# Decoder layers in f32 with seven-product pairs: one weight sum made by an accumulating transfer, wider VectorE instructions, a third such pair in the long down products

## The chip, the cores and the metric

The kernel runs on one core of a Trainium2 chip. The metric is the device time of one execution, in microseconds. Engines are named as the profile names them: PE (TensorE) with its weight loads (PEld), DVE (VectorE), ACT (ScalarE), POOL (GpSimd) and SP (SyncE). DVE, ACT, POOL and SP each work through their own instructions in order.

## The reference

Two decoder layers on one sequence of 256 tokens of width 2048, all in float32. Layer 0 mixes tokens by dilated window attention, layer 1 by multi-head latent attention; both then run a SwiGLU feed-forward block (FFN), with RMS norms ahead of each and one at the end. The change lies in the FFN:

```python
D_MODEL = 2048; SEQ = 256; FFN_HIDDEN = 5632
def swiglu(xn, w_gu, w_down):
    g, u = jnp.split(xn @ w_gu, 2, axis=-1)
    return (jax.nn.silu(g) * u) @ w_down
...
h = h + swiglu(rms_norm(h, ffn_norm_g[layer]), ffn_w_gu[layer], ffn_w_down[layer])
```

## The kernel before

**Products.** Each f32 number is split into a high part `hi` (a rounding to TensorE's fast f32 form) and a rest `lo`, and each product is three matmuls, hi x hi, hi x lo and lo x hi (`mul`, L689 to L691). Activations are split once, weights as they arrive.

**The weight stream.** `WeightStream` brings weights in units of 1 MB (128 partitions x 2048 numbers). `load` issues a unit's transfers on SP into one of three `raw` buffers; `split` casts `hi` on ACT (L167) and subtracts `lo` on DVE (L168), into one of three pairs of buffers. `next`, called as TensorE's code for a unit is written, first writes the split two units ahead and then the load that this frees a buffer for. So the order on each engine is that of the program text, and a load waits until DVE has finished with the buffer.

**Units.** A unit of the FFN is a 2 x 2 set of 512-column blocks (two blocks of the inner dimension, two output columns: gate and up, or two columns of the down product) for two 128-token halves. An "eight" makes its eight block products straight, 24 matmuls. A "seven" makes the same by a scheme of Strassen's kind from seven products, 21 matmuls, with sums of weights (`th`, `tl`, after four DVE instructions at L185 to L188 on the raw tile) and sums of activations (`forms` for the gate/up products, `forms_h` for the down products, both built by `sums`, L662 to L667). The results of the sevens of a group gather in four PSUM banks `pb` beside the accumulators `la` and `ra`, and are combined at the group's end by a copy on ACT (L718) and four adds on DVE (L721) into the tiles `gate` and `up` (`left` and `right` in `mixed`).

**Groups.** The hidden dimension (44 tiles of 128) is worked in parts of 16, 16 and 12. A part has a group of eight units for every 4 tiles of gate and up, 11 groups a layer; units 2, 4 and 6 of a group are sevens (`SEVEN`), but not in the first group of a layer. A part of 16 then has two down groups of eight units, of which 2 and 5 are sevens (`SEVEN_DOWN`); the part of 12 ends in plain products (`product`). After a gate/up group, DVE adds the accumulators to `gate` and `up` (L739), ACT makes the silu (L745) and DVE the product with `up` (L747, two instructions). The transposes of that result, eight on PE (L405), are put off by one unit (`later`), so that they stand right behind unit 0 of the next group. After a down group DVE adds into `h` (L763), and POOL issues two accumulating transfers of 512 KB that add `left` and `right` to `h` (L766). POOL does nothing else in the FFN but two powers of norms (L420).

`across` (L434 to L439) turns a per-token factor into a row, once or twice a layer, by way of a diagonal tile.

Of the kernel before, what the change touches and what calls it, by code (L numbers as in the profile page):

```python
# [45 lines left out]


SEVEN = (2, 4, 6)
SEVEN_DOWN = {16: (2, 5), 12: ()}


def shape_constants():
# [35 lines left out]
class WeightStream:  # L88
# [81 lines left out]
    def split_blocks(self, raw, form):  # L170

        hi, lo = [self.hl_pool.tile([P, 2048], F32R, tag=n, name=n, bufs=self.ahead + 1) for n in ("hi", "lo")]
        blk = lambda t, i: t[:, i * 512:(i + 1) * 512]
# [9 lines left out]
        tt(out=b22, in0=b22, in1=b12, op=ALU.subtract)  # L185
# [37 lines left out]
def kernel(ctx, tc, consts, x, attn_norm_g, ffn_norm_g, a_w_qkv, a_w_o, kv_norm_g,  # L223
# [205 lines left out]

    def across(r, name):  # L430

        dg = tmp.tile([P, S], F32, tag="diag", name="diag", bufs=1)
        for t in range(NT):
            nc.vector.tensor_scalar(out=dg[:, t * P:(t + 1) * P], in0=ident, scalar1=r[:, t:t + 1],  # L434
                                    scalar2=None, op0=ALU.mult)
        ps = bank()
        mm(out=ps[:, :S], lhsT=ones, rhs=dg, start=True, stop=True)
        R = small.tile([P, S], F32, name=name, tag=name, bufs=1)
        nc.vector.tensor_copy(out=R, in_=ps[:, :S])  # L439
        return R  # L440

# [199 lines left out]
    def ffn(xT, rstd, finish):  # L641

        with tc.tile_pool(name="ffn", bufs=1) as fp:
# [11 lines left out]
            forms_h = fp.tile([P, 2, 2, 3, P], F32R, name="forms_h")  # L655

            def sums(x, kp, d):


                x2 = x[:, 2 * kp:2 * kp + 2, :].bitcast(F32)  # L660
                f = tmp.tile([P, 2, S], F32, tag="t1", name="f")
                nc.vector.tensor_tensor(out=f, in0=x2[:, :, 0:S], in1=x2[:, :, S:2 * S], op=ALU.add)  # L662
                (a11, a21), (a12, a22) = [[f[:, k, t * P:(t + 1) * P] for t in range(NT)] for k in range(2)]
                g = tmp.tile([P, 4, P], F32, tag="t1", name="g")
                for i, x_, y_, op in ((0, a21, a22, ALU.add), (1, g[:, 0], a11, ALU.subtract),
                                      (2, a11, a21, ALU.subtract), (3, a12, g[:, 1], ALU.subtract)):
# [12 lines left out]
            def mixed(X, pairs, seven, sums_of, left, right):  # L679
# [2 lines left out]


                la, ra = acc_tile(), acc_tile()
                pb = None
# [7 lines left out]
                for kp in range(pairs):  # L693
                    w = ws.next()
                    x = lambda t, kk: [X[:, 2 * kp + kk, o + t * P:o + (t + 1) * P] for o in (0, S)]
                    if kp in seven:
# [3 lines left out]
                            pb = [bank() for _ in range(4)]  # L700
                        y = lambda j: x(1, 0) if j == 0 else [sums_of[:, i, h, j - 1, :] for h in range(2)]
                        mul(pb[0], x(0, 0), w[:2], 1, st, sp)
                        mul(la[:, 0], x(0, 1), w[:2], 3, False, False)
                        mul(ra[:, 0], y(3), w[:2], 2, False, False)
                        mul(la[:, 1], x(1, 1), w[2:], 3, False, False)
                        mul(pb[1], y(0), w[2:], 0, st, sp)
                        mul(pb[2], y(1), w[2:], 1, st, sp)
                        mul(pb[3], y(2), w[2:], 2, st, sp)
                    else:
                        st, sp = kp == 0, kp == pairs - 1  # L710
                        for acc, n in ((la, 1), (ra, 0)):
                            for t in range(NT):
                                mul(acc[:, t], x(t, 0), w, n, st, False)
                                mul(acc[:, t], x(t, 1), w, n + 2, False, sp)
                    later.tick()
                    if seven and kp == seven[-1]:
                        u2 = fp.tile([P, 512], F32, tag="u2", name="u2")
                        nc.scalar.copy(out=left[:, 0], in_=pb[0])  # L718
                        for o, x_, y_ in ((u2, pb[2], left[:, 0]), (left[:, 1], pb[3], u2),
                                          (right[:, 0], pb[1], u2), (right[:, 1], pb[1], left[:, 1])):  # L720
                            nc.vector.tensor_tensor(out=o, in0=x_, in1=y_, op=ALU.add)  # L721
                return la, ra

            def pair_tiles():
                return [fp.tile([P, NT, 512], F32, tag=m, name=m) for m in ("gate", "up")]

            for part, (k0, n) in enumerate(FFN_PARTS):
                last = part == len(FFN_PARTS) - 1
                hT = big_tile([P, 16, 2 * S], F32R, "hT")
                for j in range(0, n, 4):  # L730
                    gate, up = pair_tiles()
                    first = k0 + j == 0
                    if first:
                        for kp in range(KD // 2):
                            later.put(kp + 3, lambda kp=kp: scaled(kp))
                    g, u = mixed(xT, KD // 2, () if first else SEVEN, forms, gate, up)
                    if not first:
                        for acc, d in ((g, gate), (u, up)):
                            nc.vector.tensor_tensor(out=d, in0=acc, in1=d, op=ALU.add)  # L739
                        g, u = gate, up  # L740
# [17 lines left out]
                for c in range(0, 0 if last else 4, 2):  # L758
                    left, right = pair_tiles()
                    accs = mixed(hT, n // 2, SEVEN_DOWN[n], forms_h, left, right)  # L760
                    for i, acc in enumerate(accs):
                        for t in range(NT):
                            nc.vector.tensor_tensor(out=chunk(t, c + i), in0=acc[:, t, :], in1=chunk(t, c + i),  # L763
                                                    op=ALU.add)
                    for i, part_sum in enumerate((left, right)):
                        nc.gpsimd.dma_start(out=h[:, :, (c + i) * 512:(c + i + 1) * 512], in_=part_sum,  # L766
                                            accum_op=ALU.add)

# [206 lines left out]
```

## Time and profile before

| | |
|---|---|
| median of 3 runs | 2673.95 us (2673.07 to 2676.16) |
| the profiled execution: span | 2672.9 us |
| PE busy | 2655.3 us, 99% |
| DVE busy | 2020.8 us, 76% |
| ACT busy | 1295.8 us, 48% |
| POOL busy | 24.9 us, 1% |
| SP's transfers (q1) | 492.64 MB, 55.2% of 16 DMA engines |
| POOL's transfers (q0) | 8.39 MB, 1.7% |

The span is the time of the one profiled execution from its first to its last recorded instruction. Timeline rows give a start in us from the span's start, a duration, the engine and line, the tiles written and read, their shape and, in brackets, the idle time ahead and what ended it. A long row of the page of groups ends in: busy us of the whole group, mean ns of one, idle time before them by releaser. Matmuls are pipelined, so each lasts longer than the step from one start to the next, and the step is what counts.

### The profile page before, as it was taken

The numbers are of one execution on the slowest core, as the hardware profiler recorded it, in microseconds if no ns is written. First come the engines' busy times: TensorE is split into PE (matmuls) and PEld (weight loads), VectorE is DVE, ScalarE is ACT, GpSimd is POOL, SyncE is SP. The second block draws the span as 40 slices with busy tenths as digits, with TensorE's granted clock in tenths as the row PEclk, the third lists the DMA queues.
The fourth block names the chain that finished last, engine by engine and source line by source line (L and its number), as shares of the span: only waits on it lengthen the run. The fifth ranks groups of instructions, "written<-read, shape, count | busy, mean of one in ns | idle before, by whom it ended". The sixth has DMA issues, their size and how long they took to land.

```text
span 2672.9 us, 32983 instructions
## 1 busy us (share of the span) xinstructions
PE 2655.3 (99%) x12938; PEld 2228.0 (83%) x12938; DVE 2020.8 (76%) x2758; ACT 1295.8 (48%) x1649; POOL 24.9 (1%) x28
## 2 busy tenths in 40 slices
PE   9999999999999999999999999999999999999998
PEld 7888888888888888888888888888888888888887
DVE  5676577477477668988998896588579978997985
ACT  5444444434444445544554454565445544554553
POOL 0000000000000000000000000000000000000000
PEclk9999999999999999999999999999999999999999
DMA  7545545554555555566566756444555576657663
GB/s 271 190 158 171 192 159 173 189 174 164 174 183 165 198 188 190 184 210 221 185 211 211 227 175 203 157 143 140 177 180 189 189 230 199 217 188 222 204 215 133
DMA packets 308091, 504.20 MB, mean 189 GB/s; under 512 B 13960, under 2 KB 117088, under 8 KB 307552
## 3 DMA queue, kind: packets, MB, share of 16 engines
q1 hardware_dynamic: 302960, 492.64, 55.2%
q0 software_dynamic: 4352, 8.39, 1.7%
q8 instruction: 101, 1.65, 0.3%
q10 hardware_dynamic: 624, 1.07, 0.1%
q14 instruction: 54, 0.44, 0.0%
HBM read 491.57 MB, written 2.10 MB: 185 GB/s over the span
## 4 chain that ended last, share of the span: by engine, by line
PE 87%; DVE 6%; DMA 3%; issue 2%; ACT 2%; SPq 0%; POOL 0%; ACTq 0%; DVEq 0%; POOLq 0%
PE acc L451 14%; PE acc L689 10%; PE acc L690 10%; PE acc L691 10%; PE acc L471 8%; PE acc L470 8%; PE acc L472 8%; PE acc L454 7%; DVE lo L168 2%; PE bank L689 2%; PE bank L691 2%; PE bank L690 2%; DMA raw<-in_ffn_w_gu_dram 1%; DMA raw<-in_ffn_w_down_dram 1%; PE bank L566 1%
## 5 line engine op out<-in xcount | busy, mean ns | idle before, releaser
L158 DVE TENSOR_TENSOR lo<-raw,hi 128x1024 fp32r<-128x1024 f32 (+2 forms) x450 | 515.7, 1166 | 347.3 <-ACT hi L157 331.3
L157 ACT CAST hi<-raw 128x1024 fp32r<-128x1024 f32 (+2 forms) x450 | 432.6, 1006 | 550.0 <-PE acc L451 297.4
L167 ACT CAST hi<-raw 128x1024 fp32r<-128x1024 f32 (+1 forms) x404 | 443.8, 1130 | 384.3 <-PE acc L691 146.4
L168 DVE TENSOR_TENSOR lo<-raw,hi 128x1024 fp32r<-128x1024 f32 (+1 forms) x404 | 526.2, 1321 | 110.0 <-ACT hi L167 108.8
L689 PE MATMUL acc<-hi,xT_f 128*128 128x512 f32 x988 | 387.2, 392 | 0.4 <-DVE gate L739 0.4
L691 PE MATMUL acc<-hi,xT_f 128*128 128x512 f32 x988 | 385.4, 390 | 0.0
L690 PE MATMUL acc<-lo,xT_f 128*128 128x512 f32 x988 | 385.0, 390 | 0.0
L451 PE MATMUL acc<-xT_a,hi 128*128 128x512 f32 x1536 | 379.4, 395 | 0.0
L451 PEld LDWEIGHTS acc<-xT_a,hi 128*128 128x128 f32 x1536 | 281.6, 188 | 53.8
L689 PEld LDWEIGHTS acc<-hi,xT_f 128*128 128x128 f32 x988 | 185.5, 188 | 41.8 <-issue 2.5
L167 ACT CAST th<-raw 128x1024 fp32r<-128x1024 f32 x152 | 154.0, 1049 | 133.4 <-DVE raw L187 122.3
L691 PEld LDWEIGHTS acc<-hi,xT_f 128*128 128x128 f32 x988 | 185.5, 188 | 39.1
L690 PEld LDWEIGHTS acc<-lo,xT_f 128*128 128x128 f32 x988 | 185.6, 188 | 38.2
L454 PEld LDWEIGHTS acc<-xT_a,lo 128*128 128x128 f32 x1536 | 196.9, 191 | 7.6
L454 PE MATMUL acc<-xT_a,lo 128*128 128x256 f32 x1536 | 199.2, 283 | 0.0
L168 DVE TENSOR_TENSOR tl<-raw,th 128x1024 fp32r<-128x1024 f32 x152 | 180.5, 1221 | 12.6 <-ACT th L167 12.4
L689 PE MATMUL acc<-hi,hT 128*128 128x512 f32 x400 | 156.4, 391 | 1.5 <-DVE gate L739 1.0
L691 PE MATMUL acc<-hi,hT 128*128 128x512 f32 x400 | 155.9, 390 | 0.0
L690 PE MATMUL acc<-lo,hT 128*128 128x512 f32 x400 | 155.8, 390 | 0.0
L471 PE MATMUL acc<-lo,xT_a 128*128 128x512 f32 x384 | 150.6, 392 | 0.8 <-DVE lo L158 0.8
L472 PE MATMUL acc<-hi,xT_a 128*128 128x512 f32 x384 | 150.9, 393 | 0.0
L470 PE MATMUL acc<-hi,xT_a 128*128 128x512 f32 x384 | 150.8, 393 | 0.0
(274 smaller groups left out, 3942.6 us busy)
## 6 DMA issues: line engine op xcount, KB each, us to landing
raw<-in_ffn_w_gu_dram SPq DMA_DIRECT2D x352, 512.0 KB, 4.5
raw<-in_a_w_qkv_dram SPq DMA_DIRECT2D x143, 1024.0 KB, 4.9
raw<-in_ffn_w_down_dram SPq DMA_DIRECT2D x128, 512.0 KB, 5.0
raw<-in_ffn_w_down_dram SPq DMA_DIRECT2D x24, 1024.0 KB, 5.1
raw<-in_a_w_o_dram SPq DMA_DIRECT2D x16, 1024.0 KB, 5.0
raw<-in_b_w_o_dram SPq DMA_DIRECT2D x16, 1024.0 KB, 5.1
raw<-in_b_w_kv_b_dram SPq DMA_DIRECT2D x8, 1024.0 KB, 5.3
raw<-in_b_w_q_b_dram SPq DMA_DIRECT2D x8, 768.0 KB, 4.5
```

The lines of the kernel that those rows point to most:

```text
L157: nc.scalar.copy(out=h, in_=src)
L158: nc.vector.tensor_tensor(out=l, in0=src, in1=h.bitcast(F32), op=ALU.subtract)
L167: self.nc.scalar.copy(out=hi, in_=src)
L168: self.nc.vector.tensor_tensor(out=lo, in0=src, in1=hi.bitcast(F32), op=ALU.subtract)
L451: mm(out=acc[:, i, :], lhsT=sl(hi, kk), rhs=xT[:, k0 + kk, :], start=first and kk == 0, stop=False)
L454: mm(out=acc[:, i, 0:S], lhsT=sl(lo, kk), rhs=xT[:, k0 + kk, 0:S], start=False, stop=last and kk == nk - 1)
L470: mm(out=acc[:, t, :ncol], lhsT=xh, rhs=rhs(hi, kk), start=st, stop=False)
L471: mm(out=acc[:, t, :ncol], lhsT=xh, rhs=rhs(lo, kk), start=False, stop=False)
L472: mm(out=acc[:, t, :ncol], lhsT=xl, rhs=rhs(hi, kk), start=False, stop=sp)
L689: mm(out=out, lhsT=xh, rhs=wh, start=st, stop=False)
L690: mm(out=out, lhsT=xh, rhs=wl, start=False, stop=False)
L691: mm(out=out, lhsT=xl, rhs=wh, start=False, stop=sp)
```

## The change

Three edits in the FFN and a small one beside them:

1. In a seven, the first weight sum is no longer made by DVE. `load` issues a third transfer on POOL (L108), which adds one 128x512 block (256 KB) from DRAM onto the first block of the raw tile as it lies in SBUF, once the first of SP's two halves has landed there. The two halves change places in SP's queue.
2. A split is one instruction of 2048 columns on ACT and one on DVE (two of 1024 before, or one of 1536 in a seven). The remaining weight sums are one DVE instruction of 512 and one of 2 x 512 columns. `th` and `tl` have 1536 columns (2048 before, in two instructions each) and serve three of the seven products; `hi` and `lo` serve four, which come first. The group's end has two adds of 512 and one of 1024 columns in place of four of 512; the tile `gate` has a third slot for a middle result, and the tile `u2` is gone.
3. In down groups of the parts of 16, units 2, 4 and 6 are sevens (2 and 5 before): 84 sevens in place of 76.
4. `across` builds its diagonal in the tile of its result.

```diff
-SEVEN_DOWN = {16: (2, 5), 12: ()}
+SEVEN_DOWN = {16: (2, 4, 6), 12: ()}
...
-                for n in range(2):
+                for n in (1, 0):
                     self.nc.sync.dma_start(out=v[:, :, 1 - n, :], in_=ap[n])
+                if form == "seven":
+                    self.nc.gpsimd.dma_start(out=v[:, 0, 0, :], in_=ap[0][:, 0, :], accum_op=ALU.add)
...
+        self.halve(hi, lo, raw)
         if form == "eight":
-            for i in (slice(0, 1024), slice(1024, 2048)):
-                self.halve(hi[:, i], lo[:, i], raw[:, i])
             return hi, lo
-        i = slice(512, 2048)
-        self.halve(hi[:, i], lo[:, i], raw[:, i])
-        th, tl = [self.sum_pool.tile([P, 2048], F32R, tag=n, name=n, bufs=1) for n in ("th", "tl")]
-        b12, b11, b22, b21 = [blk(raw, j) for j in range(4)]
-        tt = self.nc.vector.tensor_tensor
-        tt(out=b22, in0=b22, in1=b12, op=ALU.subtract)
-        tt(out=b12, in0=b12, in1=b11, op=ALU.subtract)
-        tt(out=b11, in0=b11, in1=b22, op=ALU.add)
-        tt(out=b21, in0=b21, in1=b11, op=ALU.subtract)
-        for i in (slice(0, 1024), slice(1024, 2048)):
-            self.halve(th[:, i], tl[:, i], raw[:, i])
+        th, tl = [self.sum_pool.tile([P, 1536], F32R, tag=n, name=n, bufs=1) for n in ("th", "tl")]
+        v = raw.rearrange("p (i c) -> p i c", c=512)
+        self.nc.vector.tensor_tensor(out=v[:, 2], in0=v[:, 0], in1=v[:, 2], op=ALU.subtract)
+        self.nc.vector.tensor_tensor(out=v[:, 1::2], in0=v[:, 1::2],
+                                     in1=v[:, 2].unsqueeze(1).broadcast_to([P, 2, 512]), op=ALU.subtract)
+        self.halve(th, tl, raw[:, 512:])
...
                         mul(pb[0], x(0, 0), w[:2], 1, st, sp)
-                        mul(la[:, 0], x(0, 1), w[:2], 3, False, False)
-                        mul(ra[:, 0], y(3), w[:2], 2, False, False)
-                        mul(la[:, 1], x(1, 1), w[2:], 3, False, False)
-                        mul(pb[1], y(0), w[2:], 0, st, sp)
+                        mul(la[:, 0], x(0, 1), w[:2], 3, first("la0"), False)
+                        mul(pb[1], y(0), w[:2], 0, st, sp)
+                        mul(ra[:, 0], y(3), w[:2], 2, first("ra0"), False)
+                        mul(pb[3], y(2), w[2:], 0, st, sp)
                         mul(pb[2], y(1), w[2:], 1, st, sp)
-                        mul(pb[3], y(2), w[2:], 2, st, sp)
+                        mul(la[:, 1], x(1, 1), w[2:], 2, first("la1"), False)
...
-                        u2 = fp.tile([P, 512], F32, tag="u2", name="u2")
                         nc.scalar.copy(out=left[:, 0], in_=pb[0])
-                        for o, x_, y_ in ((u2, pb[2], left[:, 0]), (left[:, 1], pb[3], u2),
-                                          (right[:, 0], pb[1], u2), (right[:, 1], pb[1], left[:, 1])):
-                            nc.vector.tensor_tensor(out=o, in0=x_, in1=y_, op=ALU.add)
+                        nc.vector.tensor_tensor(out=left[:, 1], in0=pb[2], in1=left[:, 0], op=ALU.add)
+                        nc.vector.tensor_tensor(out=left[:, 2], in0=pb[3], in1=left[:, 1], op=ALU.add)
+                        nc.vector.tensor_tensor(out=right, in0=pb[1].unsqueeze(1).broadcast_to([P, NT, 512]),
+                                                in1=left[:, 1:3], op=ALU.subtract)
```

In the code with the change the lines lie a little higher: the split is L169 and L170, the two weight sums L182 and L183, the matmuls of `mul` L688 to L690, the group's end L716 to L719, the activation sums L656 to L661; L739, L745, L747 and L766 keep their numbers.

Two places in the order of the instructions show what moves. The first is DVE at the end of a gate/up group in layer 0 (`lo` and `tl` are splits of coming units, `u`, `gate` and `up` the group's results). Before:

```order
L168 TENSOR_TENSOR tl<-raw,th 128x1024 x2
L168 TENSOR_TENSOR lo<-raw,hi 128x1024 x3
L721 TENSOR_TENSOR u_8559<-bank,gate 128x512
L168 TENSOR_TENSOR lo<-raw,hi 128x1024
L721 TENSOR_TENSOR gate<-bank,u_8559 128x512
L721 TENSOR_TENSOR up<-bank,u_8559 128x512
L721 TENSOR_TENSOR up<-bank,gate 128x512
L739 TENSOR_TENSOR gate<-acc,gate 128x1024
L739 TENSOR_TENSOR up<-acc,up 128x1024
L747 SCALAR_TENSOR_TENSOR up<-up,rem,gate 128x512 x2
L168 TENSOR_TENSOR lo<-raw,hi 128x1536
```

The same end with the change:

```order
L170 TENSOR_TENSOR tl<-raw,th 128x1536
L170 TENSOR_TENSOR lo<-raw,hi 128x2048
L717 TENSOR_TENSOR gate<-bank,gate 128x512
L718 TENSOR_TENSOR gate<-bank,gate 128x512
L170 TENSOR_TENSOR lo<-raw,hi 128x2048
L719 TENSOR_TENSOR up<-bank,gate 128x1024
L739 TENSOR_TENSOR gate<-acc,gate 128x2x512
L739 TENSOR_TENSOR up<-acc,up 128x1024
L170 TENSOR_TENSOR lo<-raw,hi 128x2048
L747 SCALAR_TENSOR_TENSOR up<-up,rem,gate 128x512 x2
```

The last `lo` is that of unit 2 of the next group, a seven. Before, it stood behind the two products of L747 at all but the first of these ends in each layer; now it stands ahead of them at nine ends of each layer, all but the first and the last group's.

The second place is POOL's queue in the first down groups of layer 0 and around them. Before:

```order
L420 TENSOR_TENSOR rstd<-rsq_v,mhalf 128x2 x2
L766 DMA h<-gate 128x2x512
L766 DMA h<-up 128x2x512
L766 DMA h<-gate 128x2x512
L766 DMA h<-up 128x2x512
L766 DMA h<-gate 128x2x512
```

And with the change:

```order
L415 TENSOR_TENSOR rstd<-rsq_v,mhalf 128x2 x2
L108 DMA raw<-in_ffn_w_gu_dram 128x512 x9
L108 DMA raw<-in_ffn_w_down_dram 128x512 x4
L766 DMA h<-gate 128x2x512
L108 DMA raw<-in_ffn_w_down_dram 128x512
L766 DMA h<-up 128x2x512
L108 DMA raw<-in_ffn_w_down_dram 128x512
L108 DMA raw<-in_ffn_w_gu_dram 128x512
L766 DMA h<-gate 128x2x512
```

POOL's queue had only the transfers into `h`; now the accumulating transfers of the weights stand in it, and some of them between two transfers into `h`.

More of the change, by code (lines that the diff above doesn't have):

```diff
@@ L430, in across @@
     def across(r, name):
-        dg = tmp.tile([P, S], F32, tag="diag", name="diag", bufs=1)
+        R = small.tile([P, S], F32, name=name, tag=name, bufs=1)
         for t in range(NT):
-            nc.vector.tensor_scalar(out=dg[:, t * P:(t + 1) * P], in0=ident, scalar1=r[:, t:t + 1],
+            nc.vector.tensor_scalar(out=R[:, t * P:(t + 1) * P], in0=ident, scalar1=r[:, t:t + 1],
                                     scalar2=None, op0=ALU.mult)
         ps = bank()
-        mm(out=ps[:, :S], lhsT=ones, rhs=dg, start=True, stop=True)
-        R = small.tile([P, S], F32, name=name, tag=name, bufs=1)
+        mm(out=ps[:, :S], lhsT=ones, rhs=R, start=True, stop=True)
         nc.vector.tensor_copy(out=R, in_=ps[:, :S])
@@ L653, in ffn @@
             forms = fp.tile([P, len(SEVEN), 2, 3, P], F32R, name="forms")
-            forms_h = fp.tile([P, 2, 2, 3, P], F32R, name="forms_h")
+            forms_h = fp.tile([P, 3, 2, 3, P], F32R, name="forms_h")
             def sums(x, kp, d):
@@ L684, in mixed, with first @@
                 la, ra = acc_tile(), acc_tile()
-                pb = None
+                pb, begun = None, set()
+                def first(m):
+                    new = m not in begun
+                    begun.add(m)
+                    return new
                 def mul(out, x, w, i, st, sp):
@@ L702, in mixed @@
                         mul(pb[0], x(0, 0), w[:2], 1, st, sp)
-                        mul(la[:, 0], x(0, 1), w[:2], 3, False, False)
-                        mul(ra[:, 0], y(3), w[:2], 2, False, False)
-                        mul(la[:, 1], x(1, 1), w[2:], 3, False, False)
-                        mul(pb[1], y(0), w[2:], 0, st, sp)
+                        mul(la[:, 0], x(0, 1), w[:2], 3, first("la0"), False)
+                        mul(pb[1], y(0), w[:2], 0, st, sp)
+                        mul(ra[:, 0], y(3), w[:2], 2, first("ra0"), False)
+                        mul(pb[3], y(2), w[2:], 0, st, sp)
                         mul(pb[2], y(1), w[2:], 1, st, sp)
-                        mul(pb[3], y(2), w[2:], 2, st, sp)
+                        mul(la[:, 1], x(1, 1), w[2:], 2, first("la1"), False)
                     else:
-                        st, sp = kp == 0, kp == pairs - 1
-                        for acc, n in ((la, 1), (ra, 0)):
+                        sp = kp == pairs - 1
+                        for acc, m, n in ((la, "la", 1), (ra, "ra", 0)):
                             for t in range(NT):
-                                mul(acc[:, t], x(t, 0), w, n, st, False)
+                                mul(acc[:, t], x(t, 0), w, n, first(f"{m}{t}"), False)
                                 mul(acc[:, t], x(t, 1), w, n + 2, False, sp)
@@ L716, in mixed @@
                     if seven and kp == seven[-1]:
-                        u2 = fp.tile([P, 512], F32, tag="u2", name="u2")
                         nc.scalar.copy(out=left[:, 0], in_=pb[0])
-                        for o, x_, y_ in ((u2, pb[2], left[:, 0]), (left[:, 1], pb[3], u2),
-                                          (right[:, 0], pb[1], u2), (right[:, 1], pb[1], left[:, 1])):
-                            nc.vector.tensor_tensor(out=o, in0=x_, in1=y_, op=ALU.add)
+                        nc.vector.tensor_tensor(out=left[:, 1], in0=pb[2], in1=left[:, 0], op=ALU.add)
+                        nc.vector.tensor_tensor(out=left[:, 2], in0=pb[3], in1=left[:, 1], op=ALU.add)
+                        nc.vector.tensor_tensor(out=right, in0=pb[1].unsqueeze(1).broadcast_to([P, NT, 512]),
+                                                in1=left[:, 1:3], op=ALU.subtract)
                 return la, ra
             def pair_tiles():
-                return [fp.tile([P, NT, 512], F32, tag=m, name=m) for m in ("gate", "up")]
+                return [fp.tile([P, n, 512], F32, tag=m, name=m) for m, n in (("gate", NT + 1), ("up", NT))]
             for part, (k0, n) in enumerate(FFN_PARTS):
@@ L736, in ffn @@
                     g, u = mixed(xT, KD // 2, () if first else SEVEN, forms, gate, up)
+                    gate = gate[:, 0:3:2]
                     if not first:
@@ L764, in ffn @@
                                                     op=ALU.add)
-                    for i, part_sum in enumerate((left, right)):
+                    for i, part_sum in enumerate((left[:, 0:3:2], right)):
                         nc.gpsimd.dma_start(out=h[:, :, (c + i) * 512:(c + i + 1) * 512], in_=part_sum,
```

3 lines of the change are left out of this document (1 added, 2 removed).

## The prediction

> **What bounds the kernel now.** I read the page first, then TensorE's timeline inside a group, then the places where its steps grow long, and there the rows of the other engines.
>
> ```profile
> span 2672.9 us, 32983 instructions
> PE 2655.3 (99%) x12938; PEld 2228.0 (83%) x12938; DVE 2020.8 (76%) x2758; ACT 1295.8 (48%) x1649; POOL 24.9 (1%) x28
> ```
>
> TensorE is idle for 2672.9 - 2655.3 = 17.6 us in all. So the kernel gets shorter only by less TensorE work or by some of those 17.6 us, and longer by any new wait of TensorE. VectorE and ScalarE matter only at places where TensorE waits for them. The timeline of TensorE through a seven-product unit (from 1097.67) and the eight-product unit behind it (from 1102.50 to 1107.96):
>
> ```profile
> 1097.67 0.39 PE L689 MATMUL bank<-hi,xT_f 128*128 128x512 f32 x1
> ...
> 1099.73 0.39 PE L689 MATMUL acc<-th,xT_f 128*128 128x512 f32 x1
> ...
> 1100.42 0.40 PE L689 MATMUL bank<-th,xT_f 128*128 128x512 f32 x1
> ...
> 1101.12 0.40 PE L689 MATMUL bank<-th,forms 128*128 128x512 f32 x1
> ...
> 1102.50 0.39 PE L689 MATMUL acc<-hi,xT_f 128*128 128x512 f32 x1
> ...
> 1107.96 0.39 PE L689 MATMUL acc<-hi,xT_f 128*128 128x512 f32 x1
> ```
>
> An eight takes 5.46 us, a seven 4.83. The product of three matmuls that starts at 1100.42 takes 0.70 us until 1101.12; one of the eight takes 5.46/8 = 0.68. Next the ends of groups. The first matmul of a new group follows the last of the old one late, at 8 ends; these are the first and the last of the 8 pairs, and the transposes of one group's result:
>
> ```profile
> 1064.29 0.39 PE L691 MATMUL acc<-hi,xT_f 128*128 128x512 f32 x1
> 1064.87 0.47 PE L689 MATMUL acc<-hi,xT_f 128*128 128x512 f32 x1 [0.19 <-DVE gate L739]
> ...
> 1070.43 1.03 PE L405 MATMUL bank<-ident,up 128*128 128x128 f32 x8
> ```
> ```profile
> 2383.65 0.39 PE L691 MATMUL acc<-hi,xT_f 128*128 128x512 f32 x1
> 2384.15 0.47 PE L689 MATMUL acc<-hi,hT 128*128 128x512 f32 x1
> ```
>
> The steps are 0.58 and 0.50 us where 5.46/24 = 0.23 is usual; over the 8 the excess sums to 3.2 us. Waits on `tl` inside a seven add about 1.5 us, by the same count of long steps. The waits name both:
>
> ```profile
> PE acc L689 <- DVE gate L739: 1.4, 5, 0.4
> PE acc L690 <- DVE tl L168: 0.6, 2, 0.5
> ```
>
> They show less than the steps do, because a pipelined matmul counts as busy.
>
> **TensorE's work.** Eight more sevens (two groups of down products in each of four long parts; 24 matmuls go): 8 x (5.46 - 4.83) = **-5.0 us**. In each of the 76 sevens that stay, one product moves from `th` to `hi` weights: 0.70 - 0.68 = 0.02 us, so -1.6 if it loses all of that and -0.6 if other operands cause part of it. I take **-1.6**, since the rows with `hi` and `xT_f` are the nearest. Both are on the path, which TensorE is. No cover is needed.
>
> **VectorE and ScalarE.** The groups, by shape:
>
> ```profile
> L168 DVE TENSOR_TENSOR lo<-raw,hi 128x1024 fp32r<-128x1024 f32 x328 | 393.0, 1220 | 68.6 <-ACT hi L167 67.6
> L167 ACT CAST hi<-raw 128x1024 fp32r<-128x1024 f32 x328 | 331.4, 1050 | 284.4 <-PE acc L691 112.0 <-DMA raw<-in_ffn_w_gu_dram 76.0 <-issue 65.3
> L168 DVE TENSOR_TENSOR lo<-raw,hi 128x1536 fp32r<-128x1536 f32 x76 | 133.5, 1756 | 41.4 <-ACT hi L167 41.2
> L167 ACT CAST hi<-raw 128x1536 fp32r<-128x1536 f32 x76 | 112.4, 1479 | 99.9 <-issue 35.3 <-PE acc L691 34.4 <-DMA raw<-in_ffn_w_down_dram 20.8
> L185 DVE TENSOR_TENSOR raw<-raw 128x512 f32<-128x512 f32 x76 | 52.5, 690 | 2.1
> ```
>
> 512 more columns cost 0.54 us on VectorE and 0.43 on ScalarE, so a 2048-wide instruction is an estimated 1.756 + 0.536 = 2.29 and 1.479 + 0.429 = 1.91. A seven falls on VectorE from 1.76 + 4 x 0.69 + 2 x 1.22 = 6.96 to 2.29 + 0.69 + 1.22 + 1.76 = 5.96 us. That 1.0 us a unit is worth nothing by itself, since VectorE is not the bound; it can only remove the short waits above: **-4.7 us** (3.2 + 1.5) at most, and I take it all, because the shorter queue makes `tl` earlier and I price the group's end anew below. What the width costs is latency: an eight's first half was done after 1.05 + 1.22, and now nothing is usable before 1.91 + 2.29.
>
> The group's end, on VectorE, in a group whose TensorE steps are clean (its last seven starts on TensorE at 1310.87, the next group at 1321.16, 10.29 later):
>
> ```profile
> 1308.95 2.43 DVE L168 TENSOR_TENSOR tl<-raw,th 128x1024 fp32r<-128x1024 f32 x2
> 1312.16 2.36 DVE L168 TENSOR_TENSOR lo<-raw,hi 128x1024 fp32r<-128x1024 f32 x2 [0.78 <-ACT hi L167]
> 1314.77 1.23 DVE L168 TENSOR_TENSOR lo<-raw,hi 128x1024 fp32r<-128x1024 f32 x1 [0.25 <-ACT hi L167]
> ...
> 1319.63 1.23 DVE L739 TENSOR_TENSOR gate<-acc,gate 128x1024 f32<-128x1024 f32 x1
> ```
> ```profile
> 1310.87 0.39 PE L689 MATMUL bank<-hi,xT_f 128*128 128x512 f32 x1
> ...
> 1321.16 0.40 PE L689 MATMUL acc<-hi,xT_f 128*128 128x512 f32 x1
> ```
>
> Counted from the seven's start, the first `lo` stands at 1.29, so its cast began at about 0.24. Now that cast ends at 2.15 and the chain is: `lo` 2.20 (2.29 less the overlap of 0.08 that back-to-back rows show) to 4.35, L717 and L718 0.74 and 0.60 (the second needs the first) to 5.69, the second `lo` to 7.89, L719 1.14 to 9.03, the gate's add 1.23 to 10.26. TensorE starts 0.14 behind it (the add that ends at 1063.51 + 1.22 = 1064.73 released the matmul at 1064.87, the row is below): 10.40 against 10.29, a stall of 0.11 at each end. At the 10 ends that have no worse (8 down groups, 2 last gate/up groups) that is **+1.1 us**.
>
> Behind it comes the order. `lo` of the next group's unit 2 now stands between the up add and the two products of L747, whose result the eight transposes need right after unit 0. The trace has that order once a layer already, at the first such end (on ScalarE the silu stands behind that unit's cast):
>
> ```profile
> 1063.51 1.22 DVE L739 TENSOR_TENSOR gate<-acc,gate 128x1024 f32<-128x1024 f32 x1
> ...
> 1066.23 1.76 DVE L168 TENSOR_TENSOR lo<-raw,hi 128x1536 fp32r<-128x1536 f32 x1 [0.29 <-ACT hi L167]
> 1067.90 1.41 DVE L747 SCALAR_TENSOR_TENSOR up<-up,rem,gate 128x512 f32<-128x512 f32 x2
> ```
> ```profile
> 1064.71 1.48 ACT L167 CAST hi<-raw 128x1536 fp32r<-128x1536 f32 x1 [3.90 <-DVE gate L739]
> 1066.10 1.33 ACT L745 ACTIVATE gate<-gate,rem 128x512 f32<-128x512 f32 x2
> ```
>
> There the products end at 1069.31 and the transposes at 1070.43 are not held up. The cast starts 0.19 after the group's due start (1064.29 + 0.23 = 1064.52). With the wide forms: cast to 0.19 + 1.91 = 2.10, `lo` from 2.14 to 4.34, products 1.41 to 5.75, TensorE at 5.89; the second transpose is due at 5.44 + 0.11 = 5.55. That is 0.34 us at the 18 gate/up ends that have this order now: **+6.1 us**. Bounds: 0 if the wide forms are 0.4 us cheaper together than the line through 1024 and 1536, 0.74 x 18 = 13 if they are as much dearer.
>
> **The accumulating transfer.** That cast also waits for the sum made at load. Nearest rows are the loads and POOL's other accumulating transfers, of twice the size:
>
> ```profile
> q1 hardware_dynamic: 302960, 492.64, 55.2%
> q0 software_dynamic: 4352, 8.39, 1.7%
> ...
> raw<-in_ffn_w_gu_dram SPq DMA_DIRECT2D x352, 512.0 KB, 4.5
> ...
> h<-gate POOLq DMA_DIRECT2D x8, 512.0 KB, 6.2
> ```
> ```profile
> 1196.48 1.21 POOL L766 DMA_DIRECT2D h<-up  x1 [0.68 <-DVE h L763]
> ```
>
> 84 transfers of 256 KB add 84 x 0.262 = 22 MB, by q0's 1.7% for 8.39 MB some 4.5% of the engines beside 55.2%: room enough. The chain for unit 2 of the next group: its buffer is freed by the last seven's `tl` (above, 1308.95 + 2.43 = 1311.38, 0.5 after that seven's start); loading takes 4.5; the accumulating transfer 3.1 to 6.2 (half of and the whole of the row for 512 KB; I take 4.6, the middle, since the 1.21 of issue does not halve). That is 9.6 to 9.6 + 1.1, where the second pair of loads issued close behind another shares the engines, against 10.29 + 0.19 = 10.48 where the cast wants it. So it is level at most ends, and I put it 0.5 us late at the 8 ends of groups in which the sums of the transposed result (L656 to L661 now) also lie on VectorE ahead of `tl`: 8 x 0.5 = **+4.0 us**. Bounds 0 (3.1 us) and about +18 (6.2 us puts it 11.2 or later, 0.7 or more at 18 ends, with up to 1.1 more from the loads). Behind the waiting cast are queued the silu, and on VectorE `lo` and the products; TensorE's transposes wait for them. Units 4 and 6, whose buffers come free a unit or more before their casts want them, have 2 to 5 us by the same count, and POOL's h accumulations alternate with these. The other loads keep their order, the halves of one unit are swapped; the shorter `across` is one buffer less: nothing on the path, a few tenths if it were.
>
> The Trainium skill, page "DMA: Bandwidth & Descriptors", section "Anatomy of one DMA — SWDGE (gpsimd) path", fits such a transfer as 2.0 us plus bytes over 436e3 per us: an estimate of 2.6 us for 256 KB and 3.2 for 512 KB. The row for 512 KB has 6.2, so the trace of before speaks against it; by it the sum is early and the +4.0 is 0.
>
> **Sum.** -5.0 - 1.6 - 4.7 + 1.1 + 6.1 + 4.0 = -0.1 against the profiled span of 2672.9. The median of the runs, 2673.95, is 1.05 above that span; the forecast is 2673.9.
>
> **Rivals.** (1) The transfer is the new bound: it lands like the row of 6.2, at all 18 ends a cast waits 1 us. +18 in place of +4.0: +13.9, **2688**. For it: the only accumulating rows; a late one delays `tl`, loads and the next one. Against it: half the bytes, and a queue that is little used. It decides from 4.6 + 0.9 us on. (2) Faster: the wide forms and the order cost nothing at TensorE and the transfers are in time: -5.0 - 1.6 - 4.7 = -11.3; with a third of the 6.1 + 1.1 left, -8.9, **2665**. For it: the first such end today has 1.1 us to spare. Against it: the spare goes into the 0.53 + 0.43 of width. (3) The transfer takes 3.1 us, half the row for twice the bytes, and is early at every end, with the order as I price it: -4.1, **2670**. For it: half the bytes; against it: the issue of 1.21 us, which is not moving data. The fit of the page named above would make it this one. (4) That the change does not do what it says is out: TensorE's order has 24 rows less and POOL's 84 transfers more.
>
> **How the numbers follow.** A measurement of this kernel tells about 0.2%, 5.3 us. The forecast has 0.36 and rival 3 0.12; both lie within 2668.6 to 2679.3, so that no change has 0.48. Rival 1 and what lies between it and the forecast above 2679.3 have 0.33; rival 2 has 0.19. To hold 8 in 10 the range has to reach just past rivals 1 and 2 and leaves their far ends out: 2664 to 2690. The likeliest case's own range is 2668.6 to 2679.3.
>
> **What would show it.** Right: TensorE's seven at 4.81; L170 on 2048 columns at 2.2 to 2.3; a stall of 0.2 to 0.5 at the transposes of 18 groups, released by L747; casts of unit 2 waiting for a raw DMA. Wrong: no stall there (rival 2), or transfers of 5.5 us and more with casts that wait 1 us and longer (rival 1). It would be wrong altogether if a unit inside the groups waited for its accumulated buffer.

## The result, and the profile after

| | before | after |
|---|---|---|
| median of runs | 2673.61 us (2673.07 to 2676.16, 4) | 2742.8 us (2724.09 to 2743.84, 4) |
| profiled span | 2672.9 us | 2740.2 us |

The ratio is 1.0243, 95% interval 1.0214 to 1.0273: the change makes the kernel slower by 69 us by the medians (one of the four runs, 2724, by 50; its mean granted clock was 0.998, that of the other three 0.993 and 0.994). The forecast was 2673.9, and the range ended at 2690. The page of the kernel after, its first lines and its accumulating queue:

```profile
span 2740.2 us, 32715 instructions
PE 2673.0 (98%) x12914; PEld 2229.7 (81%) x12914; DVE 1978.5 (72%) x2390; ACT 1289.2 (47%) x1425; POOL 98.6 (4%) x112
...
L169 ACT CAST hi<-raw 128x2048 fp32r<-128x2048 f32 x240 | 458.7, 1912 | 576.3 <-DMA raw<-in_ffn_w_gu_dram 228.6
L170 DVE TENSOR_TENSOR lo<-raw,hi 128x2048 fp32r<-128x2048 f32 x240 | 549.7, 2290 | 232.3 <-ACT hi L169 231.0
L688 PE MATMUL acc<-hi,xT_f 128*128 128x512 f32 x988 | 393.3, 398 | 20.1 <-DVE gate L739 11.9
...
raw<-in_ffn_w_gu_dram POOLq DMA_DIRECT2D x60, 256.0 KB, 4.3
```

PE has 67 us of idle in place of 17.6, though it has 24 matmuls less. VectorE has 42 us less to do, and that gained nothing. The waits name three places that were shorter or absent before:

```profile
ACT hi L169 <- DMA raw<-in_ffn_w_gu_dram: 228.6, 65, 10.0
...
ACT hi L169 <- DMA raw<-in_ffn_w_down_dram: 99.2, 29, 7.3
...
PE bank L400 <- DVE up L747: 24.8, 29, 3.3
...
PE acc L688 <- DVE gate L739: 13.6, 18, 2.9
```

The same waits of casts before:

```profile
ACT hi L167 <- DMA raw<-in_ffn_w_gu_dram: 76.0, 40, 4.1
...
ACT hi L167 <- DMA raw<-in_ffn_w_down_dram: 31.0, 15, 4.4
```

Casts wait 328 us for raw tiles (107 before), the transposes wait for the products of L747, and a group's first matmul for the gate's add. I also summed, from PE's timeline, by how much each long step in the FFN exceeds the usual one. The same count is used for every run below, and a stall there is such an excess:

| us over the usual step | before | after |
|---|---|---|
| starts of groups and of units | 6.5 | 34.7 |
| transposes of a group's result | 2.1 | 33.6 |
| waits on `tl` inside a seven | 1.5 | 3.6 |
| matmuls that step 0.42 to 0.44 us | 0.4 | 8.2 |
| sum | 10.5 | 80.1 |

Of the last row, two steps, 0.4 us, are in both kernels at full clock; the other 39 of the kernel after, 7.8 us, are at half clock.

One group end of the kernel after shows the chain. First PE's timeline: the last seven starts.

```profile
1375.21 0.39 PE L688 MATMUL bank<-hi,xT_f 128*128 128x512 f32 x1
```

SP's, at the same time: the load of the next group's unit 2 is issued.

```profile
1375.24 0.88 SPq L106 DMA_DIRECT2D raw<-in_ffn_w_gu_dram  x2
```

POOL's: the accumulating transfer for that unit.

```profile
1381.86 0.86 POOL L108 DMA_DIRECT2D raw<-in_ffn_w_gu_dram  x1 [20.21 <-DMA raw<-in_ffn_w_gu_dram]
```

ACT's: the cast of that unit, and the silu of the group that ended.

```profile
1387.46 1.91 ACT L169 CAST hi<-raw 128x2048 fp32r<-128x2048 f32 x1 [6.87 <-DMA raw<-in_ffn_w_gu_dram]
1389.27 1.33 ACT L745 ACTIVATE gate<-gate,rem 128x512 f32<-128x512 f32 x2
```

VectorE's: the add for `right` (here `up`) and the accumulators' adds of the ended group, unit 2's `lo`, and the first of the two products.

```profile
1383.12 1.22 DVE L719 TENSOR_TENSOR up<-bank,gate 128x1024 f32<-128x1024 f32 x1
1384.45 1.23 DVE L739 TENSOR_TENSOR gate<-acc,gate 128x1024 f32<-128x1024 f32 x1
1385.70 1.22 DVE L739 TENSOR_TENSOR up<-acc,up 128x1024 f32<-128x1024 f32 x1
1389.40 2.29 DVE L170 TENSOR_TENSOR lo<-raw,hi 128x2048 fp32r<-128x2048 f32 x1 [2.47 <-ACT hi L169]
1391.61 0.75 DVE L747 SCALAR_TENSOR_TENSOR up<-up,rem,gate 128x512 f32<-128x512 f32 x1
```

And PE's again: the new group's first matmul, and the transposes behind its unit 0.

```profile
1385.82 0.47 PE L688 MATMUL acc<-hi,xT_f 128*128 128x512 f32 x1 [0.15 <-DVE gate L739]
...
1392.41 0.33 PE L400 MATMUL bank<-ident,up 128*128 128x128 f32 x1 [0.87 <-DVE up L747]
1393.07 0.98 PE L400 MATMUL bank<-ident,up 128*128 128x128 f32 x7 [0.33 <-DVE up L747]
```

POOL gets its half of the tile 6.6 us after the load's issue, the sum is in place 5.5 us later, and the cast starts 0.15 behind that, at 1387.46, 1.77 us after it was due (1375.21 + 10.29 + 0.19 = 1385.69). The silu has had its input since 1385.7, but stands behind that cast; the products stand behind that cast's `lo`; PE stands at the transposes until 1393.

### The profile page after: what moved, and what is told of

It is laid out like the page before. It is cut to its first block, busy times and chain, and to the rows that moved or that the text cites. A ratio compares the mean times of both kernels' runs of the same rounds, so it can differ in the third digit from the quotient of the medians.

```text
span 2740.2 us, 32715 instructions
## 1 busy us (share of the span) xinstructions
PE 2673.0 (98%) x12914; PEld 2229.7 (81%) x12914; DVE 1978.5 (72%) x2390; ACT 1289.2 (47%) x1425; POOL 98.6 (4%) x112
## 5 line engine op out<-in xcount | busy, mean ns | idle before, releaser
L169 ACT CAST hi<-raw 128x2048 fp32r<-128x2048 f32 x240 | 458.7, 1912 | 576.3 <-DMA raw<-in_ffn_w_gu_dram 228.6
L170 DVE TENSOR_TENSOR lo<-raw,hi 128x2048 fp32r<-128x2048 f32 x240 | 549.7, 2290 | 232.3 <-ACT hi L169 231.0
L688 PE MATMUL acc<-hi,xT_f 128*128 128x512 f32 x988 | 393.3, 398 | 20.1 <-DVE gate L739 11.9
L690 PE MATMUL acc<-hi,xT_f 128*128 128x512 f32 x988 | 388.4, 393 | 0.0
L688 PEld LDWEIGHTS acc<-hi,xT_f 128*128 128x128 f32 x988 | 187.9, 190 | 67.7 <-issue 27.2
L690 PEld LDWEIGHTS acc<-hi,xT_f 128*128 128x128 f32 x988 | 187.7, 190 | 41.0
L169 ACT CAST th<-raw 128x1536 fp32r<-128x1536 f32 x84 | 124.2, 1478 | 115.2 <-DVE raw L183 114.5
L170 DVE TENSOR_TENSOR tl<-raw,th 128x1536 fp32r<-128x1536 f32 x84 | 147.2, 1753 | 25.9 <-ACT th L169 25.9
L688 PE MATMUL acc<-hi,hT 128*128 128x512 f32 x344 | 135.4, 394 | 4.6 <-DVE h L763 2.9
L689 PE MATMUL acc<-lo,hT 128*128 128x512 f32 x344 | 134.3, 390 | 0.0
L690 PE MATMUL acc<-hi,hT 128*128 128x512 f32 x344 | 134.1, 390 | 0.0
```

What stands on the lines that cost most here:

```text
L169: self.nc.scalar.copy(out=hi, in_=src)
L170: self.nc.vector.tensor_tensor(out=lo, in0=src, in1=hi.bitcast(F32), op=ALU.subtract)
L688: mm(out=out, lhsT=xh, rhs=wh, start=st, stop=False)
L689: mm(out=out, lhsT=xh, rhs=wl, start=False, stop=False)
L690: mm(out=out, lhsT=xl, rhs=wh, start=False, stop=sp)
```

## The experiments

Theories at the start: the transfer itself (raw tiles come late), the order at the group's end (the ended group's work is queued behind a waiting cast), and the width (VectorE gets no part of a `lo` before the whole cast is done). Ratios are against the kernel before, whose median lay between 2672.5 and 2673.4 beside these runs; each stands with its 95% interval.

**The sum on VectorE.** In the kernel after:

```diff
-                    self.nc.gpsimd.dma_start(out=v[:, 0, 0, :], in_=ap[0][:, 0, :], accum_op=ALU.add)
...
+        if form == "seven":
+            self.nc.vector.tensor_tensor(out=raw[:, :512], in0=raw[:, :512], in1=raw[:, 512:1024], op=ALU.add)
         self.halve(hi, lo, raw)
```

> The kernel after, with the first weight sum made by VectorE (one 512-wide add) in place of the accumulating transfer; wide instructions, third seven and the order at the group ends stay. If the transfer is the cause (it makes each seven's raw buffer ready some 5 us later, 0.56 of waiting and 4.1 to 7 of transfer), nearly all of the 69 us go: 2665 to 2678, and the longest stalls at group starts are below 1 us. If the wide instructions at the group ends are the cause, it stays above 2700.

Measured: 2703.25 us, 1.0109 (1.0092 to 1.0126). Neither expectation: 40 us go, 30 stay. The stalls at transposes are back at 2.1 us; those at starts stay at 32.1, and their long steps last 0.9 to 1.9 us. Casts now wait for VectorE's sum (L176), and PE for the gate's add in VectorE's queue at the group's end:

```profile
ACT hi L167 <- DVE raw L176: 121.1, 30, 7.5
...
PE acc L688 <- DVE gate L739: 18.9, 18, 1.6
```

So the transfer costs more than the sum that it replaced, and it is not the only cost.

**The order at the group's end.** The cast and `lo` of unit 2 pinned behind the silu and the products, with the transfers kept:

```diff
...
+        a = self.nc.scalar.copy(out=hi, in_=src)
+        b = self.nc.vector.tensor_tensor(out=lo, in0=src, in1=hi.bitcast(F32), op=ALU.subtract)
+        if self.pin:
+            for ins in (a, b):
+                self.tc.keep_in_program_order(ins)
+            self.pin = False
...
```

> The kernel after, transfers and all, but the cast and the rest of the next group's unit 2 are kept behind the ended group's silu and products on ScalarE and VectorE. If the lateness costs only because the silu and the products are queued behind a cast that waits for the transfer, the 33.6 us of stalls at the transposes and most of the 8 us at half clock behind them go: 2700 or less. If the transfers make the ring of three raw buffers too slow, the 35 us of stalls at group starts stay or take up what is won: 2720 to 2745.

Measured: 2709.76 us, 1.014 (1.0119 to 1.0161). 33 us go, about what the stalls at the transposes lose (33.6 to 2.1). The stalls at starts stay at 36.5, as the second expectation has it for them; the time lies between the two.

**Both.** The two edits together:

> Both edits: sum on VectorE and unit 2 behind the silu and the products. The order at the 18 ends was priced at 6.1 us (0.34 each): 6 us below the run with the sum on VectorE alone, about 2664. If that order costs nothing by itself, no difference between the two.

Measured: 2704.37 us, 1.0117 (1.0102 to 1.0132), the same as with the sum alone. So the order costs nothing by itself; it costs with a cast ahead that is as late as the transfer makes it.

**The third seven alone.** The kernel before with `SEVEN_DOWN = {16: (2, 4, 6), ...}`, the larger `forms_h` and the smaller diagonal:

> The kernel before with sevens at 2, 4 and 6 of the long down groups and the smaller diagonal of across (for room), nothing else. By the TensorE term alone (8 x 0.63): 2668.6. If the third seven overloads VectorE or the loads in the down groups, 2674 or above.

Measured: 2669.62 us, 0.9986 (0.9976 to 0.9995), span 2668.1. The term for PE's work holds: -3.4 by the medians, -4.8 by the spans, -5.0 forecast.

**The width, taken out of the run with VectorE's sums**, and taken out of the kernel after:

```diff
-        self.halve(hi, lo, raw)
+        for i in (slice(0, 1024), slice(1024, 2048)):
+            self.halve(hi[:, i], lo[:, i], raw[:, i])
```

> The run with the sum on VectorE, with the hi and lo split in two instructions of 1024 columns again, for eights and sevens. If the 30 us that are left there are the width (a lo of 2048 cannot start before its whole cast is done, and the adds that release the next group stand behind two of them), the group starts fall back to about 0.2 us of stall and the time to 2668 to 2680. If they are the weight sum or the shape of the evacuation on VectorE, it stays at 2695 or above.

> The kernel after, transfers and all, with the hi and lo split in two instructions of 1024 columns. If width and transfer add up, it gains what the run above gains on its own parent, 25 to 33 us: 2710 to 2718, and the order at the group ends, which this also puts back, takes it to 2690 or so. If the transfers' lateness sets everything, it stays within 10 us of 2743.

Measured: 2692.34 us, 1.0073 (1.0058 to 1.0088), 11 us less than its parent; and 2721.91 us, 1.0188 (1.0171 to 1.0205), 21 us less than the kernel after. Each lies between its two expectations. The second run also has the products ahead of `lo`, and its stalls at transposes are 2.1 us, but those at starts are 46: the lateness moves on to the next start.

**The width, put into the kernel before** (`self.halve(hi, lo, raw)` for the eights alone):

> The kernel before, with nothing changed but that an eight is split in one instruction of 2048 columns per engine. If width by itself costs at the group ends, 0.5 to 1.4 us at each of 22: 2685 to 2705. If the width only costs together with the new sums and evacuation, 2674 within 4.

Measured: 2684.03 us, 1.0043 (1.0028 to 1.0058): 11.5 us, just below the expected 12 to 32 and the same as the width's price with VectorE's sums. Its stalls at starts go from 6.5 to 16.3 us. The order moved here too: unit 2's `lo` stands ahead of the products at 18 ends, as in the kernel after; but no transposes are held up, so that the 11.5 are the width's.

**Transfers where there was thought to be room.** Sums on VectorE at unit 2, transfers at 4 and 6:

```diff
                 if form == "seven":
-                    self.nc.gpsimd.dma_start(out=v[:, 0, 0, :], in_=ap[0][:, 0, :], accum_op=ALU.add)
+                    if self.n_seven % 3:
+                        self.nc.gpsimd.dma_start(out=v[:, 0, 0, :], in_=ap[0][:, 0, :], accum_op=ALU.add)
+                    else:
+                        self.plain.add(self.n_raw)
+                    self.n_seven += 1
...
+        if self.n_split in self.plain:
+            self.nc.vector.tensor_tensor(out=raw[:, :512], in0=raw[:, :512], in1=raw[:, 512:1024], op=ALU.add)
```

> The kernel after, with the transfer kept at units 4 and 6 of a group (56 of 84) and the sum on VectorE at unit 2. If the transfer costs only at unit 2, where loads are in flight beside it and the silu is queued behind it, this is the run with all sums on VectorE: 2697 to 2706. If every transfer lengthens the ring of raw buffers, about two thirds of the 40 us between the two are left: 2720 to 2732.

Measured: 2710.53 us, 1.0139 (1.0124 to 1.0154). It lies between the two expectations: 7 us above the run with no transfer, 32 below the kernel after. So the price is at unit 2 for the most part, not shared out by count.

**The gate's add first.** VectorE's sums and halves, and the gate's add ahead of the 1024-wide add that makes `right`; it writes a fourth slot of the tile, since in place it would have to wait until that add has read:

```diff
...
-                    gate = gate[:, 0:3:2]
+                    left, gate = gate[:, 0:3:2], gate[:, 0:4:3]
...
+                        nc.vector.tensor_tensor(out=gate, in0=g, in1=left, op=ALU.add)
+                        rest()
+                        nc.vector.tensor_tensor(out=up, in0=u, in1=up, op=ALU.add)
```

> The kernel after with the sums on VectorE and halves (2692.3 above), with the gate's add ahead of the 1024-wide add that makes right (it writes a fourth slot, so that it does not wait for that add to read). If the 20 us that are left against the kernel before are VectorE's queue at the group ends, 1.3 us less at each of 22 ends of which 0.5 to 1.3 show: 2672 to 2681. If they lie elsewhere (loads, th and tl), within 5 us of 2692.

Measured: 2669.2 us, 0.9985 (0.9976 to 0.9994): 23 us less, and below the kernel before. The gate's add stands first at 18 of the 20 ends with sevens. This is the kernel after with VectorE's sums in place of the transfer, without the width, and with that order. The same order in the kernel before with three sevens; here `right`'s second half reads the gate's tile after the gate's add has written it, so that half is not what the reference computes:

> The kernel before with sevens at 2, 4 and 6 of the long down groups (2669.6 above), and with the gate's add, which frees the accumulator that the next group's first matmul waits for, ahead of the two adds that make right. If the stalls at group starts come from adds queued ahead of it on VectorE, 2 to 4 us less: 2666 to 2668. If the gate's add is late for another reason (accumulator not done, casts), no difference.

Measured: 2665.35 us, 0.9971 (0.9961 to 0.9982), 4 us below its parent, as expected. Made with all results (`gate` and `up` in one tile of four slots, one wide add for `right`):

> The kernel before with sevens at 2, 4 and 6 of the long down groups, and the gate's add ahead of the add that makes right, which is one of 1024 columns; gate and up share one tile of four slots, so that the gate's add writes none that is still to be read. All results are made. By the run with the same order 2665 to 2667, below both kernels.

Measured: 2668.89 us, 0.9982 (0.9974 to 0.9991). Below the kernel before, but a miss: it cannot be told from the 2669.62 of the third seven alone. In this run the stalls at starts are 4.9 us in place of 8.1, and those on `tl` 3.5 in place of 2.2.

**The transfer's price by itself.** The kernel after without the transfer (that line alone removed), with a quarter of it and with half. The first weight sum is then left out, or made for a part of its block:

```diff
-                    self.nc.gpsimd.dma_start(out=v[:, 0, 0, :], in_=ap[0][:, 0, :], accum_op=ALU.add)
+                    self.nc.gpsimd.dma_start(out=v[:, 0, 0, :128], in_=ap[0][:, 0, :128], accum_op=ALU.add)
```

> The kernel after with the accumulating transfer left out and nothing in its place: the first weight sum is not made. The order of all other instructions is that of the kernel after. The prediction's sum without its term for the transfer is 2670. If the wide instructions and the new evacuation cost at the group ends as the runs with the sum on VectorE say, it is 2685 to 2695, and the transfer's price is the 48 to 58 us up to 2743.

> The kernel after with the accumulating transfer cut to 128 of its 512 columns (64 KB): the first weight sum is made for a quarter of the block. If the price of the transfer is its fixed part (wait, issue, first packet), 2725 to 2742. If it is its bytes, or their contention with the loads, about three quarters of the price goes: 2695 to 2712.

> The kernel after with the accumulating transfer cut to 256 of its 512 columns (128 KB; the first weight sum is made for half of the block). On a straight line from the quarter (2690.7) to the whole (2743) this is 2708. If there is a threshold between, 2692 to 2698, or 2720 and up.

Measured: 2683.07 (1.0039, 1.0026 to 1.0053), 2690.74 (1.0067, 1.0051 to 1.0083) and 2705.3 us (1.0118, 1.0099 to 1.0137; its runs lie between 2696.7 and 2710.2). The first lies just below its range, so that the transfer costs 60 us by the medians, more than the expected 48 to 58. Its first quarter costs 8 of them; that run lies below both of its ranges. The half lies near the straight line (2708). VectorE's sum has a price too: the run with it took 2703.25, 20 us more than the run with no first sum, so of the 30 us that stayed there 10 are left to the kernel after itself. The page's issues give the transfer's time to landing, with 64 KB and with 128 KB:

```profile
raw<-in_ffn_w_gu_dram POOLq DMA_DIRECT2D x60, 64.0 KB, 2.7
```

```profile
raw<-in_ffn_w_gu_dram POOLq DMA_DIRECT2D x60, 128.0 KB, 3.2
```

and 4.3 in the kernel after. These medians hide the place that counts. By unit, from the landings of all 28 transfers each, the whole transfer takes 5.54 us (4.2 to 7.3) at unit 2 and 4.17 and 4.15 at units 4 and 6; the half 4.96, 3.11 and 3.14; the quarter 4.41, 2.67 and 2.67.

**A plain copy.** The same 256 KB on the same queue, without `accum_op=ALU.add`, so that the first weight sum is not made:

> The kernel after with the transfer of 256 KB a plain copy over the first block instead of an addition to it (the first weight sum is not made), same queue, same bytes, same waits. If the accumulating kind is what makes it long, the copy lands about 1 to 2 us sooner and the time is 2690 to 2710. If the bytes and the queue are, it lands after 4 to 7 us too and the time stays at 2730 to 2745.

Measured: 2691.6 us, 1.0071 (1.0057 to 1.0085): the first expectation. It lands after 4.59 us at unit 2 and 2.98 and 2.97 elsewhere (the page's issues, all units):

```profile
raw<-in_ffn_w_gu_dram POOLq DMA_DIRECT2D x60, 256.0 KB, 3.0
```

So the addition makes it 1.2 us longer with the same bytes, and those and the 1 us at unit 2 make 51 us of time. The copy and the quarter, which land within 0.2 us of each other at unit 2, cost the same.

**Transfers kept, the queue repaired.** Halves, the gate's add written first, and the transfers:

> The kernel after, full transfers kept, with halves of 1024 columns and the gate's add ahead of the add that makes right: the run with these two and the sums on VectorE took 2669.2. If the transfer costs because the group end's work is queued behind it, most of that is gone here: 2670 to 2685. If late raw buffers stop TensorE whatever the order, 2695 to 2715.

Measured: 2720.06 us, 1.0178 (1.0162 to 1.0193), above both expectations; but the scheduler put the add for `right` ahead again at all 20 ends, so this is the run of halves once more and tells nothing of the queue. With `keep_in_program_order` on that add:

> Full transfers, halves of 1024 columns, the gate's add pinned ahead of the add that makes right at all 20 ends: the run with VectorE's sums in place of the transfers took 2669.2. If the transfer's lateness costs only what stands in the group end's queues, 2670 to 2690. If late raw buffers stop TensorE whatever the order, 2700 to 2720.

Measured: 2703.59 us, 1.0114 (1.0099 to 1.0129): the second expectation. Against 2669.2, the run with VectorE's sums, the transfer costs 34 us in this order. The waits of casts and of PE in it:

```profile
ACT hi L169 <- DMA raw<-in_ffn_w_gu_dram: 159.8, 63, 7.3
...
ACT hi L169 <- DMA raw<-in_ffn_w_down_dram: 75.0, 29, 6.5
...
PE acc L690 <- DVE gate L743: 9.2, 8, 2.3
PE bank L691 <- DVE tl L170: 7.8, 8, 1.3
```

The run at 2669.2 has these:

```profile
ACT hi L167 <- DMA raw<-in_ffn_w_gu_dram: 87.6, 43, 3.5
ACT hi L167 <- DMA raw<-in_ffn_w_down_dram: 47.5, 23, 3.9
```

So raw tiles that are late cost in this order too: `hi` waits, `lo` and `tl` come late, and what stands behind them waits. By the count of long steps the starts have 23 us against 9, and the waits on `tl` 15 against none. What part of the 60 us was the queue's is not shown. Like against like, the transfer in place of VectorE's sum costs 40 us in the order of the kernel after (2742.8, 2703.25), 30 with halves (2721.91, 2692.34), 34 here, and 5 with unit 2's split pinned (2709.76, 2704.37); and VectorE's sum, 20 us in the order of the kernel after, was left out in no other order. The last run is the kernel after with both orders pinned:

> The kernel after (wide instructions, full transfers) with unit 2's split kept behind the silu and the products, and the gate's add ahead of the add that makes right. The first of these alone took 2709.8. Another 0.8 to 1.2 us at each of 22 group ends: 2683 to 2692, if the gate's add is late by what is queued ahead of it. If it is late because the casts behind it wait for their loads, 2700 to 2710.

Measured: 2695.88 us, 1.0083 (1.0066 to 1.01). It lies between the two; the stalls at starts are 21.3 us in place of 36.5. Order brings back 47 of the 69 us without touching a transfer.

## Why the prediction was wrong

**Where it held.** PE's work: a seven takes 4.81 us, and the third seven alone brings 3.4 to 4.8 of the forecast 5.0. The durations: 1912 and 2290 ns against 1.91 and 2.29. The places: the cast that waits for the transfer, the silu and the products behind it, the transposes behind those. A transfer of 256 KB that is alone takes 4.17 us (unit 4), the forecast 4.6.

**The step that failed: "The accumulating transfer", +4.0 us.** It is the term that was mis-sized: 55 to 60 us (the two ends from the ratios and the medians of the kernel after and the run without the transfer). At the end shown above the wait for the first half is 6.62 us from the issue of its load (forecast 4.5 to 5.6), with 0.56 between landing and POOL's start in it that no term had; the transfer takes 5.5 beside two pairs of loads (forecast 4.6); the cast is 1.8 late, not 0.5. The sign that the prediction named for rival 1, transfers of 5.5 us with casts that wait 1 us and longer, is there. The wait is there at nearly all ends, not at 8: of the 28 casts of a unit 2 in the kernel after, 26 start within 0.2 us behind their transfer's landing, those of down groups among them. The other part is the multiplier. I counted a late microsecond once per end; the cast's lateness stood once at the transposes (33.6 us, 2.1 without the transfer), once more at starts (34.7, 21.8 without the transfer), and brought PE's clock down (7.8 us, none without). Rival 1 had this mechanism and its place, and 18 us for it.

**The terms for the width, +1.1 and +6.1, and the stalls taken as gone, -4.7.** The sum without the transfer was 2670; the run without it took 2683. Of the 13 us, the width makes some 11 by two pairs of runs (10.9 with VectorE's sums, 11.5 in the kernel before); in the run without the transfer it was not taken out. It was priced at the transposes, +6.1, where it costs nothing by itself (the two runs with VectorE's sums are alike in both orders, and the run without the transfer has no stall there), and at the starts with 0.11 an end, where it showed. The gate's add started at 1384.45, 0.11 after the add for `right` ended, since it overwrites a slot that this one reads: the overlap of 0.08 that I had taken from independent rows is not there. PE started at 1385.82, 10.61 after the seven in place of 10.40, and the stall of a clean end is 0.3 and not 0.1. And the stalls of before, which I took as gone (-4.7), grew.

**What hid the gain.** VectorE lost 42 us of work and PE's busy time still grew by 18. The amount of VectorE's work was not in PE's way, its order was: in the run at 2669.2, with VectorE's sums, halves and the gate's add first, VectorE is busy for 2037.1 us, 16 more than before.

**What stays open.** The plain copy lands 0.95 us sooner at unit 2 and saves 51 us. By the count of long steps, 23 of them lie at the transposes, 13 at starts, 4 at waits on `tl` and 8 at half clock: 48 of the 49 us between the two spans. Why 0.95 us at 28 units makes that much, no run separates. The part of the clock may be larger than 8: the one run of the kernel after at 2724 had a granted clock of 0.998, but there is no trace of it.

## What to carry to other kernels

Before moving a step of a weight's preparation into its load, add up load, hand-over and transfer under the loads that run beside it, and compare with the time at which the tile is wanted at the tightest place; an average slack says nothing. Where queues are in order, a late tile costs once for everything that stands behind it: look first at what is queued behind the new wait, and put work that frees the bound engine's accumulator ahead of work that does not. Making instructions wider to save an engine that is not the bound can cost the bound engine latency.

## What the runs showed of the hardware

After a step of 3.25 us from one matmul to the next, PE ran at half clock. PE's timeline and the windows around it, of the kernel after:

```profile
1291.76 0.39 PE L690 MATMUL acc<-hi,xT_f 128*128 128x512 f32 x1
1295.01 0.47 PE L688 MATMUL acc<-hi,xT_f 128*128 128x512 f32 x1 [2.87 <-DVE gate L739]
...
1296.02 0.63 PE L688 MATMUL acc<-hi,xT_f 128*128 128x512 f32 x1
1296.45 0.63 PE L689 MATMUL acc<-lo,xT_f 128*128 128x512 f32 x1
...
1298.96 0.39 PE L689 MATMUL acc<-lo,xT_f 128*128 128x512 f32 x1
```
```profile
core 0: us, PE busy (x) PEld busy (x) DVE busy (x) ACT busy (x) POOL busy (x), PEclk, DMA share, GB/s
...
1295.00:1299.00 4.00, 3.99 (x11) 3.14 (x12) 2.33 (x2) 3.13 (x3) 0.21 (x1) 0.57 0.62 231
1299.00:1303.00 4.00, 4.00 (x24) 3.37 (x22) 3.97 (x5) 0.64 (x1) 0.65 (x1) 1.00 0.46 66
```

The matmuls step 0.43 us where 0.23 is usual, and the granted clock is 0.57 for 4 us, then 1.00. The trace has six such stretches in the FFN, in which 39 matmuls of 512 columns ran so, 7.8 us more in all. They follow steps of 2.44, 2.73, 3.01, 3.25, 3.46 and 3.64 us; but steps of 2.44, 2.55 and 3.02 us elsewhere in the same trace were followed by full clock, so the length of a stall does not settle it here. The Trainium skill, page "TensorE: Matmul & The Clock Gate", section "Why this matters for your kernels", tells to leave no gap over about 3 us. The row shown agrees; the 2.44 and the 2.73 show that a shorter gap can bring the clock down too.

An accumulating transfer of 256 KB from DRAM took 4.17 us where hardly anything moved beside it (unit 4), a plain copy of the same bytes on the same queue 2.98; beside two pairs of loads (unit 2) they took 5.54 and 4.59. The Trainium skill, page "DMA: Bandwidth & Descriptors", section "Anatomy of one DMA — SWDGE (gpsimd) path", gives 2.0 us plus bytes over 436e3 per us, an estimate of 2.6 us for this size; the copy at unit 4 is 0.4 above it and the accumulating transfer 1.6. The Trainium skill, page "Collectives: The Full Stack", section "The bandwidth ceiling: the fold count and why AG ≠ RS ≠ AR", says of the adding step of a collective that it reads two sources through one ring; the difference of 1.2 us goes that way, but no run here shows the ring.
